# Raw weight loads, the residual load and unit spacing moved; the norm root of the next block multiplied in by GpSimd

## The chip, the cores and the metric

The kernel runs on one core of a Trainium2 chip. The metric is the device time of one execution in microseconds (us). The core has five engines that take their instructions in order, each from its own queue, and meet only through semaphores: TensorE (PE: matmuls, with a separate weight load, PEld), VectorE (DVE), ScalarE (ACT), GpSimd (POOL) and SyncE (SP). SP issues nearly all DMA transfers here; POOL issues some.

## The reference

One layer over 2048 tokens of width 1024, all in float32. A first RMS norm feeds one projection. Part of its columns goes through a diagonal state-space layer (S5), part through attention over 64-frame chunks; then come an output projection with residual, a second RMS norm with a SwiGLU block, a residual and a last norm.

```python
h = rmsnorm(x, norm_mix_g)                    # x * rsqrt(mean(x*x)) * g
proj = h @ w_in                               # u_ssm | q | k | v
y_ssm = s5_mixer(u_ssm, ...)                  # 32 groups, one 64-dim complex state each
y_att = chunked_attention(q, k, v, rel_bias)  # own chunk and 8 earlier ones, 8 heads
x = x + concatenate([rmsnorm(y_ssm), rmsnorm(y_att)]) @ w_out
h2 = rmsnorm(x, norm_ffn_g)
x = x + (silu(h2 @ w_gate) * (h2 @ w_up)) @ w_down
return rmsnorm(x, norm_final_g)
```

## The kernel before

Every float32 operand of a large product is split into a high and a low part (`split`, line 154: ACT copies the high part, DVE subtracts), and three matmuls make one product (`mm3`, line 148). So each operand that TensorE reads has passed ACT and DVE first. A tile framework allocates buffers by tag (a tag with `bufs=2` has two), sets all semaphores and orders each engine's queue: an instruction may go ahead of one that stands earlier in the program when it is ready and the earlier one is not, and program order decides between ready ones. TensorE's own order is pinned to program order (`Ordered`, line 72).

The stages, in order of time: the first projection and the S5 tables (`u_phase`); attention and the S5 scan together (`att_phase`); GLU and output projection (`mix_phase`); gate and up products (`gate_up_phase`, by a seven-product Strassen-like scheme); the down product (`down_phase`, the same scheme).

**The attention stage** runs over 128 steps `s`, 32 for each block of 512 tokens (`sb`). At each step TensorE gets the scores of one head's quarter of a block, the transposes of the step two earlier and, at the end of a head, its product with v (and a rescaling). Then every `Unit` in a list is advanced. A unit is a generator spread over steps `s0` to `s1`: it does its first part `pre` steps ahead of `s0` and the others evenly after that (`Unit.advance`, line 663). There are units for

- the next block's normed input (`hT_unit`, line 702): load the columns of x (`xt`, tag `xt` with 2 buffers of one tile, or tag `raw` with 2 buffers of two tiles), multiply by gain and norm root `rsn` (line 727, DVE), high part (728, ACT), low part (729, DVE). Tiles 0 to 2 have double buffers and come in a first unit (`HTA`), tiles 3 to 7 in a second one (`HTS`) when the previous block's last projection is through with them;
- the q/k and v projections (`qk_unit`, `v_unit`). Their weights come from `load_w` (line 684): in block 0 raw from the input, split, and the parts written out to `ws` (`keep_w`); in later blocks the parts are read back from `ws`;
- the S5 scan, eight units of 4 groups (`ssm_unit`, line 557), one after the other. Each has 42 parts: 18 loads by SP (U, Bst, Tm, Vm), idle parts, the input product (line 585; TensorE, into `pj`, from U and Bst; ACT copies it to X), the scan on POOL (lines 602 to 605 and 613, 614; one chain in which each instruction needs the one before), the DMA XG by POOL's queue (636), idle parts, and the output product (line 645), which reads XG and after which U's buffer is free for the next unit.

S5 unit b stood at steps 2 + 15b to 2 + 15(b + 1). `HTA` and `HTS` are counted from the block's first step, `HTP` is the `pre` of the second unit.

**The down stage** takes groups of 3 (or 2) row tiles. For each of the seven products of a group, `operand` (line 1487) loads h and w (768 KB each) by SP, splits them, and 36 matmuls run; then DVE adds four banks to the accumulator `acc` (line 1513), which starts as the residual, read from `x1` (`load_acc`, line 1515, 4 MB for a half of the tokens, right after the first product's operands).

Of the kernel before, what the change touches and what calls it, by code (L numbers as in the profile page):

```python
# [10 lines left out]
F32R = mybir.dt.float32r  # L11
I32 = mybir.dt.int32
AF = mybir.ActivationFunctionType
ALU = mybir.AluOpType
# [35 lines left out]
SW = 15  # L50
CUT = -8, -2, 2, 7, 13, 19, 24
CUTL = -8, -2, 2, 7, 13, 19, 23
ORDER = "sptf"
# [18 lines left out]
class Ordered:  # L72


    def __init__(self, tc):
        self.tc = tc
# [20 lines left out]
def f32(ap):  # L97
    return ap.bitcast(F32)
# [55 lines left out]
def split(k, hi, lo, raw):  # L154
    nc = k.nc
    return nc.scalar.copy(hi, raw), nc.vector.tensor_tensor(lo, raw, f32(hi), op=ALU.subtract)  # L156
# [499 lines left out]
class Unit:  # L656


    def __init__(self, gen, n, s0, s1, pre=0, done=0, light=1):
        self.gen, self.n, self.s0, self.s1, self.pre, self.done = gen, n, s0, s1, pre, done  # L660
        self.room = lambda a, b: sum(light if s % 4 == LPH else 1 for s in range(a, b))

    def advance(self, s):

        if s < self.s0 - self.pre:
            return
        want = 1
        if s >= self.s0:
            want += math.ceil((self.n - 1) * self.room(self.s0, s + 1) / self.room(self.s0, self.s1) - 1e-9)
        if s >= self.s1 - 1:  # L670
            want = self.n + 1
        while self.done < want:
            self.done += 1
            if next(self.gen, self) is self:
                self.done = 1 << 30


def att_phase(k, ident, S, aw, x0, roots):

    tc, nc, io, pfs = k.tc, k.nc, k.io, k.pfs  # L680
    with ExitStack() as cx:
        hT, vts, qk, keep = {0: tuple(zip(*x0))}, {}, {}, {}

        def load_w(sb, n):

            w = k.t(aw, "w", [P, 2, 1024], F32R, bufs=WB)
            if sb == 0:
                raw = k.t(aw, "raw", [P, 1024], bufs=2)
                nc.sync.dma_start(raw[:], io["w_qk"][n] if n < 8 else io["w_v"][n - 8])
                for ins in split(k, w[:, 0], w[:, 1], raw[:]):  # L690
                    if n in (0, 4):
                        k.tc.keep_in_program_order(ins)
                keep[n] = w
            else:
                nc.sync.dma_start(f32(w[:]), S["ws"][n])
            return w[:, 0], w[:, 1]

        def keep_w(n):
            if n in keep:
# [2 lines left out]
        def hT_unit(sb, q0=0, q1=KT):  # L702
            hi, lo = hT.setdefault(sb, ([], []))
            ts = slice(sb * SB, (sb + 1) * SB)
            xts = {}

            def load(q, n=1):
                t = k.t(aw, "raw", [P, 1024], bufs=2) if n > 1 else k.t(aw, "xt", [P, SB], bufs=XB)
                nc.sync.dma_start(t[:].rearrange("p (q t) -> p q t", q=n), io["xt"][q * P : (q + n) * P, ts].rearrange("(q p) t -> p q t", p=P))
                for m in range(n):  # L710
                    xts[q + m] = t[:, m * SB : (m + 1) * SB]

            if q0 == 0:
                load(0)
                load(1)
            else:
                load(q0)
                for q in range(q0 + 1, q1, 2):
                    load(q, 2)
            for q in range(q0, q1):  # L720
                yield
                if q0 == 0 and q + 2 < q1:
                    load(q + 2)
# [3 lines left out]
                nc.vector.scalar_tensor_tensor(xt, xt, k.gm[:, q : q + 1], S["rsn"][:, ts], op0=ALU.mult, op1=ALU.mult)  # L727
                nc.scalar.copy(hi[q], xt)
                nc.vector.tensor_tensor(lo[q], xt, f32(hi[q]), op=ALU.subtract)
            yield  # L730

        def qk_unit(sb, pr):
            ws = [load_w(sb, n) for n in (pr, 4 + pr)]
            yield
            hi, lo = hT[sb]
            if (sb, pr) == (0, 0):
# [43 lines left out]
        QK_N = 1 + 2 * KT  # L780

        def v_unit(sb, fh):
            ws = [load_w(sb, 8 + 2 * r + fh) for r in range(2)]
# [143 lines left out]
        for sb in range(NSB):  # L927
            g0 = sb * 32
            C = CUT if sb < NSB - 1 else CUTL
            if sb > 0:  # L930
                if DB:
                    units.append(Unit(hT_unit(sb, 0, DB), 2 + DB, g0 + HTA[0], g0 + HTA[1], 2))
                units += [Unit(hT_unit(sb, DB), 2 + KT - DB, g0 + HTS[0], g0 + HTS[1], HTP), Unit(qk_unit(sb, 0), QK_N, g0 + C[0], g0 + C[1], 3, light=LIGHT)]
            units.append(Unit(v_unit(sb, 0), V_N, g0 + C[1], g0 + C[2], 2, light=LIGHT) if sb else Unit(v0, V_N, *V0, done=1))
            units += [ Unit(qk_unit(sb, 1), QK_N, g0 + C[2], g0 + C[3], 2, light=LIGHT),
                      Unit(qk_unit(sb, 2), QK_N, g0 + C[3], g0 + C[4], 2, light=LIGHT), Unit(v_unit(sb, 1), V_N, g0 + C[4], g0 + C[5], 2, light=LIGHT),
                      Unit(qk_unit(sb, 3), QK_N, g0 + C[5], g0 + C[6], 2, light=LIGHT)]
        for b in range(NG // GB):
            units.append(Unit(ssm_unit(k, sp, psum, S, b, k.ssm_eng), SSM_N, 2 + int(SW * b), 2 + int(SW * (b + 1)), light=SL))
        N = len(steps)  # L940
        for s in range(N + LAG + 2):
            if s == OPEN:
# [532 lines left out]
def down_phase(k, S):  # L1475
    tc, nc, io = k.tc, k.nc, k.io
    V, te = nc.vector, k.te
    with ExitStack() as cx:
# [5 lines left out]
        def bank(pool):  # L1484
            return k.t(pool, "ps", [P, 512])

        def operand(src, early=False):

            g, n = src.shape[0], src.shape[2]
            t = k.t(next(ring), "hd", [P, 2 * DG * 512], F32R)  # L1490
            hi, lo = (t[:, m * g * n : (m + 1) * g * n].rearrange("p (g c) -> p g c", g=g) for m in range(2))
            with tc.high_priority() if early else ExitStack():
                nc.sync.dma_start(f32(lo), src.rearrange("g p c -> p g c"))
            split(k, hi, lo, f32(lo))
            return hi, lo

        def group(hf, f0, g, acc, early):

            fs = slice(f0, f0 + g)
            x, y = [bank(dx) for _ in range(4)], None  # L1500
            for n, on_x, first, r, c in ((B11, 1, 1, 0, 0), (T1, 0, 1, 1, 1), (T2, 1, 0, 0, 1), (B22, 0, 0, 0, 1), (T3, 1, 0, 1, 1), (B21, 0, 1, 0, 0), (T4, 1, 0, 1, 0)):
                h = operand(S["hq"][hf, fs, n], early and n in (B11, T1))
                w = operand(S["wc"][fs, n], early and n in (B11, T1))
                if n == B11 and f0 == 0:
                    load_acc(hf, acc)
# [9 lines left out]
        def load_acc(hf, acc):  # L1515
            for i in range(KT):
                a = k.t((a0, a1)[hf], f"acc{i}", [P, HALF])
                nc.sync.dma_start(a[:], S["x1"][i * P : (i + 1) * P, hf * HALF : (hf + 1) * HALF])
                acc.append(a)

        def down(hs, ds, tiles, acc, t0, tn, end):

# [174 lines left out]
```

## Time and profile before

| | |
|---|---|
| time, median of 3 runs | 2295.97 us (2287.0 to 2296.15) |
| the profiled execution's own time | 2289.1 us |
| its span in the profile | 2287.1 us |
| mean granted TensorE clock | 0.978 |
| attention stage | about 130 to 690 us of the span |
| output projection, gate and up | to about 1831 us |
| down stage | 1831 us to the end |

In the profile, an engine's busy time leaves out what its queue does while it waits. "Idle before" an instruction is the time its engine had nothing to run, and the name behind the arrow is what ended it. "x8" is the number of instructions in the row. A name such as `pj<-XG,Vm` is output and inputs by the program's names. Rows of the table by stretches give each engine's busy time, the granted TensorE clock (1.00 is full), the busy share of the 16 DMA engines and GB/s. In the chain of waits each row has its start, its length, and what the chain ran through.

### The profile page before, as it was taken

The page shows a single profiled execution, that of the slowest core. Times are in us where ns is not written, and L with a number is a line of the kernel's source. Part 1 is how long each engine was busy: PE and PEld are TensorE (multiplying, and loading weights), DVE is VectorE, ACT ScalarE, POOL GpSimd, SP SyncE. Part 2 cuts the span into 40 slices and gives each one's busy share as a digit, 9 for nine tenths or more (in the row PEclk, how much of TensorE's full clock was granted, in tenths as well). Part 3 has the DMA queues.
Part 4 walks back from the last instruction along what each step waited for, and adds up shares of the span by engine and source line. Part 5 has one row for each costly group of instructions (what it writes and reads, how often), then busy time and mean ns, then how long its engine had stood idle before and what let it go on. Part 6 is the DMA issues. An engine that isn't in the chain of part 4 may idle for free.

```text
span 2287.1 us, 30278 instructions
## 1 busy us (share of the span) xinstructions
PE 2171.6 (95%) x10632; PEld 1830.1 (80%) x10632; DVE 1544.7 (68%) x2695; ACT 1000.6 (44%) x1654; POOL 348.7 (15%) x813
## 2 busy tenths in 40 slices
PE   8988899999996899999999999999999989999997
PEld 6777688898985788878888887888888778888886
DVE  7755565555556766876776678666666477789776
ACT  6444555455557652343333335333333343344322
POOL 2245765455660000000000000000000000000000
PEclk9998999999998999999999999999999999999999
DMA  8767886666644534854465567555423297465552
GB/s 299 236 221 220 257 223 201 187 188 179 188 132 124 171 121 147 267 189 151 160 200 178 167 211 258 203 169 188 139 96 110 78 341 252 166 212 193 206 189 74
DMA packets 215256, 428.33 MB, mean 187 GB/s; under 512 B 38592, under 2 KB 61168, under 8 KB 208000
## 3 DMA queue, kind: packets, MB, share of 16 engines
q1 hardware_dynamic: 210368, 412.50, 55.3%
q0 software_dynamic: 4736, 13.91, 2.0%
q8 instruction: 83, 1.36, 0.2%
q14 instruction: 69, 0.57, 0.1%
HBM read 286.86 MB, written 129.00 MB: 182 GB/s over the span
## 4 chain that ended last, share of the span: by engine, by line
PE 80%; DVE 6%; DMA 4%; POOL 4%; issue 3%; ACT 1%; SPq 1%; DVEq 0%; POOLq 0%; ACTq 0%
PE X L79 20%; PE ps L79 19%; PE Y L79 10%; PE pf L79 9%; PE big L79 9%; PE W L79 5%; PE pj L79 4%; PE sc L79 2%; PE pt L82 2%; DMA xt<-in_xp 1%; DMA hd<-wc 1%; POOL X L605 1%; DVE lo L156 1%; POOL X L604 1%; POOL st L602 1%
## 5 line engine op out<-in xcount | busy, mean ns | idle before, releaser
L79 PE MATMUL X<-hi,c 128*128 128x512 f32 x1408 | 451.0, 391 | 6.9 <-DVE c L156 5.4
L79 PE MATMUL ps<-hd,hd 128*128 128x512 f32 (+1 forms) x1968 | 430.8, 381 | 6.1 <-ACT hd L156 4.5
L79 PEld LDWEIGHTS ps<-hd,hd 128*128 128x128 f32 x1968 | 358.0, 189 | 77.7 <-ACT hd L156 5.3
L79 PEld LDWEIGHTS X<-hi,c 128*128 128x128 f32 x1408 | 265.3, 189 | 63.4 <-DVE c L156 6.3
L79 PE MATMUL X<-lo,c 128*128 128x512 f32 x704 | 274.9, 391 | 0.0
L156 ACT CAST hd<-hd 128x1536 fp32r<-128x1536 f32 (+1 forms) x106 | 147.7, 1393 | 236.3 <-DMA hd<-hq 178.7
L79 PE MATMUL Y<-hi,c 128*128 128x512 f32 x704 | 224.7, 390 | 1.5 <-DVE u L1389 1.5
L156 DVE TENSOR_TENSOR hd<-hd 128x1536 fp32r<-128x1536 f32 (+1 forms) x106 | 174.4, 1646 | 29.1 <-ACT hd L156 28.4
L156 DVE TENSOR_TENSOR c<-S,c 128x512 fp32r<-128x512 f32 x176 | 121.0, 689 | 98.3 <-ACT c L156 98.0
L1385 ACT COPY u<-X 128x512 f32<-128x512 f32 x132 | 77.4, 587 | 200.7 <-PE X L79 200.7
L1513 DVE TENSOR_TENSOR acc<-acc,ps 128x512 f32<-128x512 f32 x196 | 130.9, 684 | 50.3 <-PE ps L79 47.8
L156 ACT CAST c<-S 128x512 fp32r<-128x512 f32 x176 | 109.4, 622 | 120.1 <-PE Y L79 61.6
L79 PE MATMUL pf<-hi,w 128*128 128x512 f32 x416 | 153.9, 422 | 8.4 <-ACT w L156 4.7
L79 PE MATMUL big<-m,woh 128*128 128x512 f32 x512 | 161.2, 396 | 0.0
L79 PEld LDWEIGHTS Y<-hi,c 128*128 128x128 f32 x704 | 132.5, 188 | 29.9 <-DVE u L1389 2.2
L79 PEld LDWEIGHTS X<-lo,c 128*128 128x128 f32 x704 | 132.8, 189 | 27.5
L156 ACT CAST c<-raw 128x512 fp32r<-128x512 f32 x132 | 82.3, 623 | 150.5 <-PE Y L79 68.5
L79 PE MATMUL Y<-lo,c 128*128 128x512 f32 x352 | 137.2, 390 | 0.0
L868 DVE TENSOR_TENSOR ptl<-pt,pth 128x640 fp32r<-128x640 f32 (+3 forms) x152 | 98.3, 647 | 47.5 <-ACT pth L867 45.9
L852 ACT ACTIVATE s<-s,mn 128x640 f32<-128x640 f32 (+4 forms) x128 | 98.0, 765 | 65.6 <-DVE mn L849 61.1
L867 ACT CAST pth<-pt 128x640 fp32r<-128x640 f32 (+3 forms) x152 | 83.8, 551 | 95.6 <-PE pt L82 91.5
L79 PE MATMUL W<-hi,c 128*128 128x512 f32 x352 | 115.5, 389 | 0.0
(441 smaller groups left out, 4169.9 us busy)
## 6 DMA issues: line engine op xcount, KB each, us to landing
w<-wss SPq DMA_DIRECT2D x36, 1024.0 KB, 6.0
hq<-g SPq DMA_DIRECT2D x140, 256.0 KB, 2.1
hd<-hq SPq DMA_DIRECT2D x42, 768.0 KB, 4.5
hd<-wc SPq DMA_DIRECT2D x42, 768.0 KB, 6.0
raw<-in_w_gate SPq DMA_DIRECT2D x44, 512.0 KB, 3.8
raw<-in_w_up SPq DMA_DIRECT2D x44, 512.0 KB, 4.3
wc<-px SPq DMA_DIRECT2D x66, 256.0 KB, 3.2
wss<-w SPq DMA_DIRECT2D x12, 1024.0 KB, 5.7
```

Source lines behind the costliest of these rows:

```text
L79: return self.tc.keep_in_program_order(self.tc.nc.tensor.matmul(*a, **b))
L82: return self.tc.keep_in_program_order(self.tc.nc.tensor.transpose(*a, **b))
L156: return nc.scalar.copy(hi, raw), nc.vector.tensor_tensor(lo, raw, f32(hi), op=ALU.subtract)
L602: eng.tensor_tensor(t[:, :, :, :n], src, ar, op=ALU.mult)
L604: eng.tensor_tensor(dst, dst, t[:, :, :, :n], op=ALU.add)
L605: eng.tensor_tensor(dst, dst, t2[:, :, :, :n], op=ALU.add)
L852: nc.scalar.activation(s[:, :nk], s[:, :nk], AF.Exp, bias=mn[:], scale=-1.0, accum_out=sums[sb, pr][:, hh, qp : qp + 1])
L867: nc.scalar.copy(pth[:, a:b, qp, :], pt[:, a:b, :])
L868: nc.vector.tensor_tensor(ptl[:, a:b, qp, :], pt[:, a:b, :], f32(pth[:, a:b, qp, :]), op=ALU.subtract)
L1385: nc.scalar.copy(u[:], ps[:])
L1513: V.tensor_tensor(a, a, ps[:], op=ALU.add)
```

## The change

Five things change together.

1. Block 0's q/k and v weights: the raw loads move to a part of their own, 4 steps ahead of the unit in place of 2; the split stays 2 steps ahead (`mid=2`).
2. The S5 units' spacing: `SU` in place of 15 steps each.
3. The next block's input: POOL multiplies by `rsn` (a part of its own for tiles 3 to 7, 2 steps ahead); ACT makes the high part with the gain as its scale; DVE makes the low part as (x times gain) minus high. DVE's first multiplication goes.
4. The loads for it: the first unit starts 3 steps earlier, the second unit's loads stand 5 steps ahead in place of 2.
5. The down stage: in the first group of each half, a product's operands are loaded one product ahead, and `acc` is loaded in four quarters, each ahead of the product that first adds to it. In the very first group the operands are issued by POOL's queue (`aside`).

```diff
-HTA = -12, -9
+HTA = -15, -12
-HTP = 2
+HTP = 5
-SW = 15
+SU = 2, 19, 35, 49, 64, 78, 93, 107, 122
 class Unit:
-        want = 1
+        want = 1 if self.mid is None or s < self.s0 - self.mid else 2
         if s >= self.s0:
-            want += math.ceil((self.n - 1) * self.room(...) / ...)
+            want += math.ceil((self.n - want) * self.room(...) / ...)
+        def load_ws(sb, ns):
+            raws = [load_raw(n) for n in ns] if sb == 0 else []
+            if raws and ns not in ((0, 4), (8, 10)):
+                yield
...
 def hT_unit
+            def norm(q):
+                nc.gpsimd.tensor_tensor(xts[q], xts[q], S["rsn"][:, ts], op=ALU.mult)
...
+                yield
+                for q in range(q0, q1):
+                    norm(q)
...
-                nc.vector.scalar_tensor_tensor(xt, xt, k.gm[:, q : q + 1], S["rsn"][:, ts], op0=ALU.mult, op1=ALU.mult)
-                nc.scalar.copy(hi[q], xt)
-                nc.vector.tensor_tensor(lo[q], xt, f32(hi[q]), op=ALU.subtract)
+                nc.scalar.activation(hi[q], xt, AF.Copy, scale=k.gm[:, q : q + 1])
+                nc.vector.scalar_tensor_tensor(lo[q], xt, k.gm[:, q : q + 1], f32(hi[q]), op0=ALU.mult, op1=ALU.subtract)
...
-            units.append(Unit(ssm_unit(...), SSM_N, 2 + int(SW * b), 2 + int(SW * (b + 1)), light=SL))
+            units.append(Unit(ssm_unit(...), SSM_N, SU[b], SU[b + 1], light=SL))
...
 def operand
-                nc.sync.dma_start(f32(lo), src.rearrange("g p c -> p g c"))
+                (nc.gpsimd if aside else nc.sync).dma_start(f32(lo), src.rearrange("g p c -> p g c"))
 def group
+            if f0 == 0:
+                acc += [k.t((a0, a1)[hf], f"acc{i}", [P, HALF]) for i in range(KT)]
+                load(0)
+            for m, (n, on_x, first, r, c) in enumerate(order):
+                load(m + 1 if f0 == 0 else m)
+                if f0 == 0 and (r, c) not in seen:
+                    seen.add((r, c))
+                    load_acc(hf, acc, r, c)
...
-                nc.sync.dma_start(a[:], S["x1"][i * P : (i + 1) * P, hf * HALF : (hf + 1) * HALF])
+                nc.sync.dma_start(acc[i][:, c * 512 : (c + 1) * 512], S["x1"][i * P : (i + 1) * P, cs])
```

More of the change, by code (lines that the diff above doesn't have):

```diff
@@ L656, with __init__ @@
 class Unit:
-    def __init__(self, gen, n, s0, s1, pre=0, done=0, light=1):
-        self.gen, self.n, self.s0, self.s1, self.pre, self.done = gen, n, s0, s1, pre, done
+    def __init__(self, gen, n, s0, s1, pre=0, done=0, light=1, mid=None):
+        self.gen, self.n, self.s0, self.s1, self.pre, self.done, self.mid = gen, n, s0, s1, pre, done, mid
         self.room = lambda a, b: sum(light if s % 4 == LPH else 1 for s in range(a, b))
@@ L682, in att_phase, with load_raw @@
         hT, vts, qk, keep = {0: tuple(zip(*x0))}, {}, {}, {}
[L684 to L696, printed above, removed]
+        def load_raw(n):
+            raw = k.t(aw, "raw", [P, 1024], bufs=2)
+            nc.sync.dma_start(raw[:], io["w_qk"][n] if n < 8 else io["w_v"][n - 8])
+            return raw
+        def load_ws(sb, ns):
+            raws = [load_raw(n) for n in ns] if sb == 0 else []
+            if raws and ns not in ((0, 4), (8, 10)):
+                yield
+            ws = []
+            for i, n in enumerate(ns):
+                w = k.t(aw, "w", [P, 2, 1024], F32R, bufs=WB)
+                if raws:
+                    for ins in split(k, w[:, 0], w[:, 1], raws[i][:]):
+                        if n in (0, 4):
+                            k.tc.keep_in_program_order(ins)
+                    keep[n] = w
+                else:
+                    nc.sync.dma_start(f32(w[:]), S["ws"][n])
+                ws.append((w[:, 0], w[:, 1]))
+            return ws
         def keep_w(n):
@@ L719, in hT_unit @@
                     load(q, 2)
+                yield
+                for q in range(q0, q1):
+                    norm(q)
             for q in range(q0, q1):
                 yield
-                if q0 == 0 and q + 2 < q1:
-                    load(q + 2)
+                if q0 == 0:
+                    if q + 2 < q1:
+                        load(q + 2)
+                    norm(q)
                 xt = xts[q]
@@ L726, in hT_unit @@
                     v.append(k.t(aw, f"{n}{q}x" if q < DB and sb % 2 else f"{n}{q}", [P, SB], F32R)[:])
-                nc.vector.scalar_tensor_tensor(xt, xt, k.gm[:, q : q + 1], S["rsn"][:, ts], op0=ALU.mult, op1=ALU.mult)
-                nc.scalar.copy(hi[q], xt)
-                nc.vector.tensor_tensor(lo[q], xt, f32(hi[q]), op=ALU.subtract)
+                nc.scalar.activation(hi[q], xt, AF.Copy, scale=k.gm[:, q : q + 1])
+                nc.vector.scalar_tensor_tensor(lo[q], xt, k.gm[:, q : q + 1], f32(hi[q]), op0=ALU.mult, op1=ALU.subtract)
             yield
         def qk_unit(sb, pr):
-            ws = [load_w(sb, n) for n in (pr, 4 + pr)]
+            ws = yield from load_ws(sb, (pr, 4 + pr))
             yield
@@ L782, in v_unit @@
         def v_unit(sb, fh):
-            ws = [load_w(sb, 8 + 2 * r + fh) for r in range(2)]
+            ws = yield from load_ws(sb, (8 + fh, 10 + fh))
             yield
@@ L1485, in bank, with operand @@
             return k.t(pool, "ps", [P, 512])
-        def operand(src, early=False):
+        def operand(src, early=False, aside=False):
             g, n = src.shape[0], src.shape[2]
@@ L1499, in group, with load @@
             fs = slice(f0, f0 + g)
+            order = (B11, 1, 1, 0, 0), (T1, 0, 1, 1, 1), (T2, 1, 0, 0, 1), (B22, 0, 0, 0, 1), (T3, 1, 0, 1, 1), (B21, 0, 1, 0, 0), (T4, 1, 0, 1, 0)
             x, y = [bank(dx) for _ in range(4)], None
[L1501 to L1505, printed above, removed]
+            ops = {}
+            def load(m):
+                if m < len(order):
+                    n = order[m][0]
+                    soon = early and n in (B11, T1)
+                    ops[n] = operand(S["hq"][hf, fs, n], soon, early), operand(S["wc"][fs, n], soon, early)
+            if f0 == 0:
+                acc += [k.t((a0, a1)[hf], f"acc{i}", [P, HALF]) for i in range(KT)]
+                load(0)
+            seen = set()
+            for m, (n, on_x, first, r, c) in enumerate(order):
[3 more added lines that the diff above has]
+                    load_acc(hf, acc, r, c)
+                h, w = ops.pop(n)
                 if not on_x and first:
@@ L1513, in group, with load_acc @@
                     V.tensor_tensor(a, a, ps[:], op=ALU.add)
[L1515 to L1519, printed above, removed]
+        def load_acc(hf, acc, r, c):
+            for i in range(4 * r, 4 * r + 4):
+                cs = slice(hf * HALF + c * 512, hf * HALF + (c + 1) * 512)
+                nc.sync.dma_start(acc[i][:, c * 512 : (c + 1) * 512], S["x1"][i * P : (i + 1) * P, cs])
         def down(hs, ds, tiles, acc, t0, tn, end):
```

11 lines of the change are left out of this document (5 added, 6 removed).

## The prediction

> **What bounds the kernel now.** I read the page first, then the chain of waits through the attention stage, the busy time by stretches, and the timelines at TensorE's idle times.
>
> ```profile
> span 2287.1 us, 30278 instructions
> PE 80%; DVE 6%; DMA 4%; POOL 4%; issue 3%; ACT 1%; SPq 1%; DVEq 0%; POOLq 0%; ACTq 0%
> ```
>
> TensorE carries the chain for 80% of the span; what an edit here can win lies in the other fifth. GpSimd is in it, though the kernel as a whole hardly uses it. The chain says where; its rows are start, length, what:
>
> ```profile
> 158.78 1.73 PE pj L79 x8
> 162.85 0.51 POOL st L602
> 205.53 1.21 POOL XG L636 x2
> 206.74 24.57 issue
> 274.60 6.93 DMA XG<-X
> 292.56 5.74 DMA U<-u
> 300.04 1.13 PE pj L79 x4
> 348.86 3.47 PE pj L79 x16
> 423.22 3.45 PE pj L79 x16
> ```
>
> From 162.85 to 274.60 the chain doesn't run through TensorE. It runs through POOL's scan of S5 unit 0, then that of unit 1, then XG's transfer; then it waits for unit 2's load of U, which can't start before unit 1's output product has freed the buffer. The 24.57 us called "issue" are POOL with nothing to do until unit 1's input product. So the first three units form a loop of their own: input product (X), scan, XG, output product (Y), loads, X. TensorE's order is pinned, so it waits where it comes to Y or X too early:
>
> ```profile
> 173.01 0.79 PE L79 MATMUL pf<-hi,w 128*128 128x512 f32 x1 [4.67 <-ACT w L156]
> 193.50 0.87 PE L82 MATMUL pt<-ident,s 128*128 128x128 f32 x3 [3.36 <-DVE ptl L868]
> 212.53 0.67 PE L79 MATMUL pj<-XG,Vm 128*128 128x256 f32 x2 [1.68 <-DMA XG<-X]
> 252.30 0.50 PE L79 MATMUL pf<-hi,w 128*128 128x512 f32 x1 [3.15 <-ACT hi L728]
> 364.46 0.89 PE L79 MATMUL pj<-U,Bst 128*128 128x256 f32 x3 [3.00 <-DMA Tm<-kts]
> 411.87 0.69 PE L82 MATMUL pt<-ident,s 128*128 128x128 f32 x2 [3.80 <-DVE ptl L868]
> ```
>
> The bracket is TensorE's idle time and what ended it. The idle times at 173, 193, 252 and 411 are those that the change goes for: block 0's split weights, and the next block's input. But after those at 173 and 193 TensorE still came 1.68 us too early for XG at 212.53: what they cost was time it would have waited anyway. Only from X3 (364.46) on does TensorE set the pace.
>
> **The change, part by part.** The sum is made against the profiled execution's own 2289.1 us (span 2287.1); the median of the three runs, 2295.97, is 6.9 above it, and the result is given against that median.
>
> *Spacing.* A unit's 42 parts are dealt out by `Unit.advance`: X are parts 9 and 10, Y 41 and 42. By its formula X stood in steps 4, 19, 34, 49, 64... (both parts) and Y in 16, 31, 46, 61, 76...; now X is in 4 and 5, 21 and 22, 37, 51, 66, 80, 95, 109 and Y in 18, 34, 48, 63, 77, 92, 106, 121. While the loop sets the time, that moves work of TensorE into its waits: X3 comes two steps later in the work. A step costs (348.86 - 300.04) / 12 = 4.07 us, from unit 2, in which TensorE had no idle time: -8.1. Against it, scans 0 and 1 start a step later, as their second part does. A step of block 0 is (212.53 - 158.78 - 4.67 - 3.36 - 1.68 - 6.9) / 12 = 3.1 us, where 6.9 is lost to the half clock after the first two idle times (8 us at a mean of 0.57 each):
>
> ```profile
> 172.00:180.00 8.00, 6.95 (x20) 5.28 (x21) 3.60 (x6) 2.91 (x7) 7.53 (x13) 0.57 0.71 255
> ```
>
> The row is one stretch: its length, the busy time of PE, PEld, DVE, ACT and POOL with their instructions, the granted clock, the share of the DMA engines and GB/s. So +6.2, and together -1.9.
>
> *Raw weights* (173, 193) and the idle time at 252 gone: 4.67 + 3.36 + 6.9 and some 7 us with the clock. All of it lies before Y0 or Y1, which the scans hold: TensorE would reach step 18 near 202, and XG can't be there before 216 (the old 158.78 to 213, a step later). I take 0. What is late next is XG. The eight or so loads of weights that move ahead on SP (0.44 us each by the median of line 709's raw loads, below) pass stores that nobody near waits for; the wait at Y0 hides them too, and without it they would cost 2 to 4 us.
>
> *Unit 4 and 6* have 11 steps from X to Y in place of 12.
>
> ```profile
> 482.64 1.21 POOL L636 DMA_DIRECT2D XG<-X  x2 [0.30 <-POOL X L614]
> 490.26 0.59 PE L79 MATMUL pj<-XG,Vm 128*128 128x256 f32 x2
> DMA to landing us min/median/max: 2.4/4.6/7.9
> ```
>
> The last row is that of all XG transfers. With its median, unit 4's XG was there 490.26 - 482.64 - 1.21 - 4.6 = 1.8 us ahead; 4.07 us less leaves a wait of 2.3. Unit 6 I put between this and unit 3 (6.5 ahead, below), at 0.5: +2.8.
>
> *The norm root on POOL*: 24 instructions of 128x512 that the trace doesn't have.
>
> ```profile
> L614 POOL TENSOR_TENSOR X<-X,fx 128x434 f32<-128x434 f32 x32 | 35.3, 1104 | 2.1
> L727 DVE SCALAR_TENSOR_TENSOR raw<-raw,g_mix,rsn 128x512 f32<-128x512 f32 x12 | 12.0, 1027 | 0.5 <-DMA raw<-in_xt 0.5
> L727 DVE SCALAR_TENSOR_TENSOR xt<-xt,g_mix,rsn 128x512 f32<-128x512 f32 x12 | 9.0, 764 | 8.8 <-DMA xt<-in_xt 8.8
> L709 SPq DMA_DIRECT2D xt<-in_xt x12: 332/426/1372, 207.4 to 398.2; - x12
> L709 SPq DMA_DIRECT2D raw<-in_xt x6: 426/440/1423, 242.6 to 398.6; - x6
> ```
>
> By size, 1104 x 512 / 434 gives 1.30 us each, 31 us on POOL for 21 us off DVE. The Trainium skill, GPSIMD Engine Reference, section 3.1, puts a two-input instruction at about 2.6 cycles an element at 1.2 GHz; an estimate from it is 1.1 us for 512, with which the sum would be 2 us lower.
>
> Where they run matters more. The loads show it: block 3's last ones went out at 398.6, though their place in the program is step 86; between step 49 (X3, 364.46) and step 61 (Y3, 423.22) that time is step 56. So they go out when a buffer comes free, not at their step, and moving them three or more steps ahead moves only block 1's, which wait for the raw buffers of block 0. The norms will follow them as DVE's did (214.6 to 408.5 for line 727). POOL's scan is one chain, and a ready instruction of lower rank can slip in between its links. Block 1's eight fall between scans 0 and 1: 0 lost, and DVE's nine multiplications no longer run beside scan 1, which was slow:
>
> ```profile
> 227.00:283.00 56.00, 44.95 (x230) 36.93 (x231) 31.88 (x75) 28.63 (x74) 40.74 (x88) 0.94 0.80 246
> 300.00:349.00 49.00, 48.84 (x297) 43.91 (x298) 32.93 (x57) 29.46 (x58) 37.82 (x88) 1.00 0.80 246
> 364.00:424.00 60.00, 53.47 (x285) 47.01 (x286) 41.23 (x65) 32.26 (x64) 40.17 (x88) 0.91 0.69 211
> 642.00:691.00 49.00, 46.51 (x296) 42.53 (x297) 26.08 (x49) 26.95 (x56) 34.98 (x88) 0.97 0.47 131
> ```
>
> Column six is POOL's busy time for the same 88 instructions: 40.74 in unit 1, 34.98 in unit 7. Between 0 and -5.8 I take -3. Block 2's: three in the pause, five inside scan 2 (+6.5; -1 for less disturbance): +5.5, all paid, as the loop holds there. Block 3's: seven inside scan 3 (9.1, less 2.6 of the 5.2 that 40.17 lies over 34.98): 6.5.
>
> *The idle time at 411* was DVE's, whose line 727 held up line 868; gone, it frees 3.80 and about 3.4 of half clock, 7.2. In unit 3 XG's last issue started at 411.43; landed by the median that is 416.7, 6.5 ahead of Y3 at 423.22. The norms use these 6.5 up, and TensorE then waits for XG the 7.2 that it gained: 0.
>
> ```profile
> 411.43 0.63 POOL L636 DMA_DIRECT2D XG<-X  x1 [0.30 <-POOL X L614]
> L728 ACT CAST hi<-raw 128x512 fp32r<-128x512 f32 x12 | 7.2, 616 | 3.6 <-DVE raw L727 3.4
> L446 ACT ACTIVATE hi<-xt,g_mix 128x512 fp32r<-128x512 f32 x16 | 11.0, 716 | 7.9 <-DMA xt<-in_xp 7.9
> ```
>
> *Loads and splits.* Block 1's three transfers now stand ahead of unit 1's 18 loads in SP's queue, on the loop: between 3 x 0.43 and 3 x 1.4 us, I take +2. ACT's scaled form costs 0.10 us more a tile (716 against 616), five tiles at each of three handovers: +1.5. Nothing waits behind the new norms on POOL but the scan and XG.
>
> *The down stage.*
>
> ```profile
> 1831.56 5.88 SPq L1518 DMA_DIRECT2D acc<-x  x8
> 1837.58 0.44 SPq L1493 DMA_DIRECT2D hd<-hq  x1
> 1852.12 1.22 PE L79 MATMUL ps<-hd,hd 128*128 128x512 f32 x2 [2.70 <-ACT hd L156]
> 1853.91 1.65 PE L79 MATMUL ps<-hd,hd 128*128 128x512 f32 x3 [0.57 <-DVE hd L156]
> 1831.00:1850.00 19.00, 16.90 (x72) 13.36 (x72) 10.68 (x12) 4.66 (x4) 0.00 (x0) 1.00 1.03 393
> 1850.00:1859.00 9.00, 6.31 (x15) 4.53 (x16) 7.11 (x6) 6.75 (x6) 0.00 (x0) 0.62 1.05 408
> ```
>
> The third product's operands queue behind 4 MB of residual, with all DMA engines busy (1.03). Loading a quarter (1 MB) first and the operands one product ahead takes out 2.70 + 0.57 and the half clock (9 us at 0.62: 3.4), -6.7. POOL's queue may bring the first operands later or not at all later; I take +1: -5.7. The Trainium skill, Trainium Kernel Development and Optimization, section Key Constraints, says that queues share the same 16 DMA engines and a second queue saves issue time alone; by it the gain is the order of the bytes, which the share of 1.03 agrees with, and POOL's queue adds 0.
>
> Sum: -1.9 + 0 + 2.8 - 3 + 5.5 + 0 + 2 + 1.5 - 5.7 = +1.2 us: 2290.3 for the profiled execution, 2297 against the median.
>
> **Rivals.**
>
> *The pauses take the norms* (faster). A pause of POOL like that of 24.57 us holds 8 x 1.30 us. If all norms fall there and the scans calm down to unit 7's: -1.9 + 2.8 - 5.8 - 2.8 (37.82 to 34.98) - 7.2 (scan 3 is then 5.2 shorter, so Y3 doesn't wait) + 0 + 1.5 - 6.7 = -20: 2276. Against it: the loads go out during scans 2 and 3.
>
> *The scan pays* (slower). A norm stands in POOL's queue ahead of the scan's next link and waits for its transfer, as DVE did (8.8 us in three waits, line 727's row). With half of that in each of scans 2 and 3 and no calming: -1.9 + 2.8 + 0 + (6.5 + 4.4) + (9.1 + 4.4 - 6.5 = 7.0, and 3.4 of half clock) + 4.2 + 1.5 - 5.7 = +22: 2318. It decides from where scans 2 and 3 grow by some 10 us more than the 12 above. For it: these loads are the ones that landed late. The Trainium skill's GPSIMD Engine Reference, section 4.1, tells to keep elementwise work on VectorE, which points the same way.
>
> *The plain reading*: every idle time named is won, 14.9 + 7 + 7.2 + 6.7 = 36: 2260. The chain speaks against it.
>
> **How the numbers follow.** Forecast 0.43, pauses 0.21, scan pays 0.31, plain reading 0.05. 0.5% (11.5 us) is about what a measurement of this kernel can tell from no change. The forecast's own spread is 2286 to 2308; it gives 0.37 within, 0.03 on each side. The pauses give 0.19 faster, 0.02 within; the scan 0.29 slower, 0.02 within; the plain reading 0.05 faster. So 0.27, 0.41, 0.32. The range 2275 to 2319 takes in both rivals' values and leaves out the plain reading and what lies beyond them, under 0.2.
>
> **What would show it.** Right: idle times at 173, 193, 252 and 411 gone or small, and in their place waits of `pj<-XG,Vm` for XG at Y0 (over 8 us), Y1 and Y2; norms between lines 602 and 614 in scans 2 and 3; no idle time over 1 us between the down stage's second and third product. Wrong: Y0 to Y2 without waits (then the loop was shorter than I think, and the plain reading gains), scans of about 35 us throughout, or an idle time of POOL inside a scan that a transfer of x ends.

## The result and the profile after

| | kernel before | changed kernel |
|---|---|---|
| median, run beside each other | 2296.15 us (2282.42 to 2302.85, 7 runs) | 2307.29 us (2300.44 to 2311.63, 7 runs) |
| ratio, with its 95% interval | | 1.0056 (1.0036 to 1.0076) |
| ratio, measured a second time, with other runs of both | | 1.0066 (1.0044 to 1.0087) |

The change costs 11 to 15 us. The forecast was +1; 2307 lies in the range of 2275 to 2319, but on the slow side of the 0.5% that the prediction called no change.

The profiled executions differ by more, 2309.9 against 2289.1 us. They were granted different clocks, 0.974 and 0.978. A second profile of the changed kernel was granted 0.978, took 2299.2 us, and so compares better. By stage, from the first rows of `sc<-hi2x,hi0x`, `pf<-gh,wgh` and `ps<-hd,hd` and the span (the attention stage runs here up to the first GLU product, some 25 us further than in the table of the kernel before):

| us | before (0.978) | changed (0.974) | changed, second profile (0.978) |
|---|---|---|---|
| attention stage | 132.40 to 714.56: 582.2 | 134.20 to 736.58: 602.4 | 131.46 to 731.16: 599.7 |
| from there to the down product | 1116.9 | 1119.1 | 1114.3 |
| down stage to the end | 455.6 | 452.4 | 451.9 |

The loss is in the attention stage, 17 to 20 us; the down stage gains 3 to 4. Single traces scatter by some us: the stages between these two, which the change leaves as they were, took 1114.3 to 1120.9 us in the fourteen traces of this document, and two kernels with the same attention stage took 582.2 and 578.3 us for it. The page of the changed kernel, its span and its chain by engine:

```profile
span 2308.1 us, 30358 instructions
PE 72%; POOL 7%; DVE 6%; issue 5%; DMA 4%; ACT 1%; SPq 1%; DVEq 0%; POOLq 0%; ACTq 0%
```

TensorE carries 72% of the chain in place of 80%, GpSimd 7% in place of 4%. The chain through the attention stage (start, length, what) says where:

```profile
212.53 1.29 POOL xt L722
246.09 3.36 issue
354.02 20.82 issue
415.86 1.29 POOL xt L722
417.93 5.86 DVE lo1x L744
428.79 41.76 issue
508.17 6.74 DMA XG<-X
```

The two long rows called issue (354.02 and 428.79) are POOL with nothing to do until the next unit's input product. The new norm (line 722) is in the chain itself, and around 416 us the chain goes from the norm into `lo1x` on DVE. `lo1x` is the low part of tile 1 of block 3, which TensorE doesn't read before step 88 of the 128. TensorE was at step 59 then. TensorE's idle times in the changed kernel:

```profile
171.62 0.44 PE L82 MATMUL pt<-ident,s 128*128 128x128 f32 x2 [3.20 <-DVE ptl L883]
215.27 0.67 PE L79 MATMUL pj<-XG,Vm 128*128 128x256 f32 x2 [3.75 <-POOL xt L722]
235.25 2.04 PE L79 MATMUL pj<-U,Bst 128*128 128x256 f32 x4 [5.51 <-DMA Tm<-kts]
426.06 1.33 PE L82 MATMUL pt<-ident,s 128*128 128x128 f32 x5 [22.74 <-DVE ptl L883]
515.04 1.19 PE L79 MATMUL pj<-XG,Vm 128*128 128x256 f32 x2 [5.26 <-DMA XG<-X]
```

At 173, 193 and 252 us the old idle times are gone or smaller, and waits for XG and for unit 1's tables stand in their place, as forecast. (The bracket at 215.27 names the norm that POOL ran just then; by the trace the third of XG's four transfers landed at 215.03.) What was not forecast is one idle time of 22.74 us where 3.80 had been (the old one at 411). Up to step 58 the changed kernel is 4.7 us ahead; at step 60 it is 14.2 us behind. The three other engines over that stretch (start, length, engine, line, instruction; in brackets the idle time before it and what ended it), POOL first:

```profile
413.30 1.04 POOL L614 TENSOR_TENSOR X<-X,fx 128x434 f32<-128x434 f32 x1
414.63 1.21 POOL L636 DMA_DIRECT2D XG<-X  x2 [0.30 <-POOL X L614]
415.86 2.50 POOL L722 TENSOR_TENSOR xt<-xt,rsn 128x512 f32<-128x512 f32 x2
418.30 4.92 POOL L722 TENSOR_TENSOR raw<-raw,rsn 128x512 f32<-128x512 f32 x4
417.17 0.72 ACT L743 ACTIVATE hi1x<-xt,g_mix 128x512 fp32r<-128x512 f32 x1 [20.45 <-POOL xt L722]
417.80 0.81 ACT L867 ACTIVATE s<-s,mn 128x640 f32<-128x640 f32 x1
417.93 5.85 DVE L744 SCALAR_TENSOR_TENSOR lo1x<-xt,g_mix,hi1x 128x512 fp32r<-128x512 f32 x1 [19.22 <-ACT hi1x L743]
423.70 0.74 DVE L744 SCALAR_TENSOR_TENSOR lo2x<-xt,g_mix,hi2x 128x512 fp32r<-128x512 f32 x1
425.18 0.82 DVE L883 TENSOR_TENSOR ptl<-pt,pth 128x640 fp32r<-128x640 f32 x1
```

Read it from the top. POOL is in scan 3 until XG's last issue at 414.63, and the next instruction in its queue is block 3's norm. ACT's queue had reached `hi1x`, which needs that norm, and stood there for 20.45 us. Behind it in the same queue were the exponential of the scores (line 867) and the high part of the transposes (line 882), which were needed at once. DVE stood 19.22 us at `lo1x`, with `ptl` (line 883) three places behind it. TensorE waited for `ptl`. When the norm came, `lo1x` took 5.85 us for what takes 0.74 us one row below, while POOL's four norms of `raw` ran beside it. The price by stretches (length; busy time of PE, PEld, DVE, ACT, POOL; granted clock; DMA share; GB/s):

```profile
402.00:426.00 24.00, 1.33 (x10) 1.03 (x8) 8.01 (x5) 3.91 (x7) 20.00 (x26) 0.61 0.14 29
426.00:432.00 6.00, 5.93 (x21) 5.06 (x21) 3.48 (x8) 2.10 (x4) 1.29 (x1) 0.55 1.02 301
515.00:522.00 7.00, 6.96 (x23) 5.84 (x24) 0.56 (x1) 1.17 (x2) 0.00 (x0) 0.63 0.05 11
```

In the first 24 us POOL works almost alone. The 6 us after it run at a clock of 0.55, which costs 2.7 us more. The third row is the half clock after the wait at unit 4's output product (515.04), 2.6 us of 7.

The order of the queues shows that this is not chance. The order is written when the kernel is built: behind scan 0's last XG issue stand 8 norms, behind scan 1's 8, behind scan 2's 1, behind scan 3's 7. Not one of the 24 stands inside a scan. So the scans were not disturbed by them; they became shorter. Scans 1 to 3, before and then changed, 88 instructions each:

```profile
231.20:275.60 44.40, 35.39 (x176) 28.59 (x175) 29.48 (x66) 23.15 (x60) 40.54 (x88) 0.92 0.79 251
304.20:345.60 41.40, 41.40 (x247) 37.02 (x247) 29.60 (x51) 24.86 (x48) 37.58 (x88) 1.00 0.85 263
368.70:412.40 43.70, 37.81 (x217) 33.55 (x216) 34.11 (x52) 23.71 (x45) 39.92 (x88) 0.95 0.75 238
```

```profile
244.80:285.20 40.40, 36.44 (x228) 32.73 (x226) 22.79 (x58) 21.98 (x59) 36.54 (x88) 0.96 0.84 257
313.90:352.50 38.60, 38.00 (x250) 34.78 (x249) 24.29 (x44) 23.42 (x46) 34.74 (x88) 1.00 0.78 239
374.80:415.85 41.05, 26.19 (x150) 22.63 (x148) 18.62 (x30) 16.43 (x30) 37.26 (x88) 0.90 0.64 194
```

POOL's busy time fell from 40.54, 37.58 and 39.92 us to 36.54, 34.74 and 37.26. DVE's first multiplication, which is gone, explains a part of it. With the norm back on DVE and the new spacing kept (the first experiment) scans 1 and 3 take 39.15 and 39.77 us, so its share there is 2.6 and 2.5; scan 2 takes 34.77, as without it (34.74). With the spacing alone scan 2 takes 35.11: it is the spacing that made this one shorter.

In the down stage, the idle time of 2.70 us ahead of the third product and the half clock after it are gone. The timeline has two idle times left there, both inside the first product; the stretches over the first three products follow, at a clock of 1.00 in place of 0.62:

```profile
1856.31 0.50 PE L79 MATMUL ps<-hd,hd 128*128 128x512 f32 x1 [0.23 <-DVE hd L156]
1858.58 7.76 PE L79 MATMUL ps<-hd,hd 128*128 128x512 f32 x33 [1.77 <-DVE hd L156]
```

```profile
1855.00:1874.00 19.00, 17.00 (x74) 13.55 (x73) 16.71 (x16) 5.93 (x4) 6.08 (x8) 1.00 1.04 411
1874.00:1883.00 9.00, 9.00 (x42) 7.44 (x41) 7.56 (x7) 4.45 (x3) 1.52 (x2) 1.00 1.04 416
```

### The profile page after: what moved, and what is told of

Same layout as the page of the kernel before. It is cut to its first block, busy times and chain, and to the rows that moved or that the text cites. A ratio compares the mean times of both kernels' runs of the same rounds, so it can differ in the third digit from the quotient of the medians.

```text
span 2308.1 us, 30358 instructions
## 1 busy us (share of the span) xinstructions
PE 2172.7 (94%) x10632; PEld 1830.1 (79%) x10632; DVE 1530.8 (66%) x2671; ACT 1002.5 (43%) x1654; POOL 383.6 (17%) x851
## 4 chain that ended last, share of the span: by engine, by line
PE 72%; POOL 7%; DVE 6%; issue 5%; DMA 4%; ACT 1%; SPq 1%; DVEq 0%; POOLq 0%; ACTq 0%
PE X L79 19%; PE ps L79 17%; PE Y L79 10%; PE big L79 8%; PE pf L79 7%; PE W L79 5%; PE pj L79 3%; PE sc L79 1%; POOL X L605 1%; PE pt L82 1%; POOL X L604 1%; POOL X L614 1%; POOL st L602 1%; POOL st L603 1%; DMA hd<-wc 1%
## 5 line engine op out<-in xcount | busy, mean ns | idle before, releaser
L1507 POOL DMA_DIRECT2D hd<-hq x7 | 5.3, 764 | 1136.8 <-PE X L79 1123.1
```

## The experiments

Three theories. **A**: ACT and DVE stand at the high and low parts of a later block, because these wait for norms that POOL takes up only after its scan. **B**: the spacing costs, by unit 4's 11 steps. **C**: the norms' own time on POOL lengthens the scans. Ratios are to the kernel before, run on the same chip, with 95% intervals.

| kernel | ratio | interval |
|---|---|---|
| parts 1, 2, 5: norm on DVE as before | 1.0015 | 0.9999 to 1.0031 |
| parts 3, 4 alone: norm on POOL | 1.0191 | 1.0166 to 1.0216 |
| changed, block 3 on DVE | 0.9986 | 0.9971 to 1.0001 |
| part 5 alone: down stage | 0.9968 | 0.9953 to 0.9984 |
| changed, ACT's order of block 3 pinned | 1.0082 | 1.0068 to 1.0097 |
| changed, 12 steps for units 4 and 6 | 1.0055 | 1.0042 to 1.0067 |
| part 1 alone: raw weights | 1.0020 | 1.0006 to 1.0033 |
| part 2 alone: spacing | 1.0025 | 1.0009 to 1.0041 |
| changed, again | 1.0066 | 1.0044 to 1.0087 |
| changed, block 3 on DVE, 12 steps | 0.9971 | 0.9956 to 0.9985 |
| the same with the raw weights as before | 0.9988 | 0.9973 to 1.0002 |
| parts 2 and 5 with 12 steps | 0.9977 | 0.9961 to 0.9993 |

**The norm back on DVE.** `hT_unit`, its loads and `HTA`, `HTP` as before; the rest changed.

```diff
-                nc.gpsimd.tensor_tensor(xts[q], xts[q], S["rsn"][:, ts], op=ALU.mult)
...
-                nc.scalar.activation(hi[q], xt, AF.Copy, scale=k.gm[:, q : q + 1])
...
+                nc.vector.scalar_tensor_tensor(xt, xt, k.gm[:, q : q + 1], S["rsn"][:, ts], op0=ALU.mult, op1=ALU.mult)
+                nc.scalar.copy(hi[q], xt)
...
```

> The changed kernel with parts 3 and 4 undone: the next block's input is multiplied by DVE in one instruction with the gain, and its loads stand where they stood before. Raw weights, spacing and down stage stay changed. Theory A (ACT and DVE stand behind POOL): the changed kernel's one idle time of 22.74 us of TensorE at 426 is gone and some 2.7 us of half clock after it, an idle time of about 4 us by DVE's multiplication comes back: 2307 - 22.7 - 2.7 + 4 = about 2286, that is 10 below the kernel before. Theory B (the spacing costs: unit 4's 11 steps): the wait for XG of 5.26 us at unit 4's output product and its half clock stay, and the norm was worth little: 2303 to 2307. Theory C (norms lengthen the scans and XG): not more than 5 us gained, and scans 2 and 3 shorter than the 35.6 and 37.9 us of busy time with the norm on POOL.

Measured 2292.52 us, ratio 1.0015: 0.4% below the changed kernel. The 22.74 us are gone; an idle time of 2.48 us stands at 407.69. That is less of a gain than theory A's 10 us below the kernel before: the wait for XG at unit 4 (4.54 us at 499.05) stayed, as theory B says, and unit 0's output product waited 9.07 us. Theory C falls: with the norm back on DVE, scans 1 and 3 are longer, not shorter, and scan 2 is the same. Scans 1 to 3:

```profile
240.80:283.80 43.00, 33.96 (x184) 28.83 (x183) 27.26 (x63) 21.90 (x57) 39.15 (x88) 0.88 0.77 254
313.80:352.40 38.60, 36.29 (x234) 32.80 (x233) 24.10 (x41) 21.64 (x42) 34.77 (x88) 1.00 0.74 229
376.70:420.30 43.60, 37.52 (x203) 31.94 (x202) 34.66 (x54) 25.48 (x49) 39.77 (x88) 0.96 0.76 232
```

**The norm alone on POOL.** The opposite edit, made in the kernel before.

```diff
...
+                nc.gpsimd.tensor_tensor(xts[q], xts[q], S["rsn"][:, ts], op=ALU.mult)
...
```

> The kernel before with parts 3 and 4 alone: norm on POOL, loads three steps further ahead. Theory A: an idle time of TensorE of about 20 us near 410 to 430 us, with ACT's queue standing at the high part of block 3's second tile: 2296 + 20 + 2 less the 3.80 us at 411 and its half clock = about 2311. Theory B: no loss, 2293 to 2297, as the units keep their 12 steps. Theory C: scans 1 to 3 longer by 5 us and more, 2300 to 2306, and no single idle time over 8 us in the attention stage.

Measured 2334.6 us, ratio 1.0191: 44 us, three times theory A's number. Theory A had counted one stall. With the old spacing there are three, one for each block. TensorE's rows, then ACT's at the second and third:

```profile
260.00 0.44 PE L79 MATMUL sc<-k,q2h 128*128 128x128 f32 x1 [17.38 <-issue]
358.42 1.33 PE L82 MATMUL pt<-ident,s 128*128 128x128 f32 x5 [22.23 <-DVE ptl L875]
451.00 1.33 PE L82 MATMUL pt<-ident,s 128*128 128x128 f32 x5 [13.44 <-DVE ptl L875]
356.21 0.72 ACT L735 ACTIVATE hi<-xt,g_mix 128x512 fp32r<-128x512 f32 x1 [23.21 <-POOL xt L714]
448.65 0.72 ACT L735 ACTIVATE hi1x<-xt,g_mix 128x512 fp32r<-128x512 f32 x1 [15.85 <-POOL xt L714]
```

Block 2's norms now stood behind scan 2, not behind scan 1, and ACT waited 23.21 us for the first of them. Block 1's last five had been put inside scan 1; at the first stall ACT waited 6.27, 4.38 and 2.55 us for norms of that block, with `k`, which TensorE missed, behind them in its queue. So the other parts of the changed kernel hide two of three such stalls: there the norms of blocks 1 and 2 stand directly behind scans 0 and 1. That it is the spacing that does this, by units 1 and 2 being later, fits the order but was not tested by itself.

**Block 3 on DVE.** POOL still does blocks 1 and 2.

```diff
+                if sb == NSB - 1:
+                    nc.vector.scalar_tensor_tensor(xt, xt, k.gm[:, q : q + 1], S["rsn"][:, ts], op0=ALU.mult, op1=ALU.mult)
+                    nc.scalar.copy(hi[q], xt)
+                    nc.vector.tensor_tensor(lo[q], xt, f32(hi[q]), op=ALU.subtract)
+                    continue
```

> The changed kernel, but the last block's input (eight tiles, needed some 140 us after the stall) is multiplied by DVE as before; POOL still does blocks 1 and 2. Theory A: the stall at 426 goes with these eight tiles alone, for it was their high parts that stood at the head of ACT's queue: about 2284 to 2288. If instead block 2's tiles, normed by POOL after scan 1, are what TensorE misses there: about 2307, as the changed kernel. Theory B: 2303 to 2307.

Measured 2288.56 us, ratio 0.9986, in the range that theory A gave. Eight of 24 tiles account for the whole loss, 0.7%, about 16 us. Where 22.74 us had been, and at ACT's same instruction:

```profile
406.94 0.77 PE L82 MATMUL pt<-ident,s 128*128 128x128 f32 x5 [2.48 <-DVE ptl L889]
400.76 0.60 ACT L746 CAST hi1x<-xt 128x512 fp32r<-128x512 f32 x1
```

ACT makes `hi1x` at 400.76 with no idle time before it.

**The down stage alone.**

```diff
...
+            load(m + 1 if f0 == 0 else m)
...
+                    load_acc(hf, acc, r, c)
...
```

> The kernel before with part 5 alone (the down stage's loads). The trace of the changed kernel shows 7 us less of lost time between 1815 and 1860 us: by that 2296 - 7 = 2289. Rival: the order of loads only moves the wait to a later product or to the end of the stage: 2294 to 2297.

Measured 2282.84 us, ratio 0.9968, that is -7.3 us (-10.8 to -3.7); the two medians differ by 5.5. The stage from its first product to the end took 451.8 us against 455.6. In the nine other traces with the edit it took 451.5 to 452.4, in three more without it 456.1 to 457.0. So the stage itself shows 3 to 6 us. In this pair of traces another 3.9 us lie in the attention stage, which the edit doesn't touch; the gain is shown, its size only to within the interval.

**ACT's order pinned.** All norms stay on POOL; ACT takes block 3's high parts at their own place in the program.

```diff
-                nc.scalar.activation(hi[q], xt, AF.Copy, scale=k.gm[:, q : q + 1])
+                ins = nc.scalar.activation(hi[q], xt, AF.Copy, scale=k.gm[:, q : q + 1])
+                if sb == NSB - 1:
+                    k.tc.keep_in_program_order(ins)
```

> The changed kernel with one thing more: ACT takes the eight high parts of the last block at their own place in the program and not earlier. POOL still makes all 24 norms, at the same places of its queue as far as scan 3 goes. Theory A (what costs is that ACT's queue, and DVE's behind it, stands at block 3's high parts while POOL scans): the idle time of 22.74 us at 426 goes, though the norms run where they ran: 0.4% to 0.8% under the changed kernel's 1.0056, so a ratio to the kernel before of 0.996 to 1.001. Rival (the norms' own time on POOL, or their running beside DVE): the ratio stays at 1.004 to 1.007.

Measured 2308.66 us, ratio 1.0082. By the number, theory A missed. The trace says why: the stall at 426 did go (TensorE's idle times over 1.2 us leap from 390 to 441), but another of 20.73 us came two scans later. The edit did more than it was meant to: two norms had moved with their high parts, from behind scan 3 to between the last links of scan 5 in POOL's queue. ACT stood at the high part that needs the first of them:

```profile
540.12 1.26 POOL L722 TENSOR_TENSOR xt<-xt,rsn 128x512 f32<-128x512 f32 x1
541.41 0.72 ACT L743 ACTIVATE hi2x<-xt,g_mix 128x512 fp32r<-128x512 f32 x1 [22.45 <-POOL xt L722]
542.17 0.75 DVE L746 SCALAR_TENSOR_TENSOR lo2x<-xt,g_mix,hi2x 128x512 fp32r<-128x512 f32 x1 [20.95 <-ACT hi2x L743]
544.43 1.33 PE L82 MATMUL pt<-ident,s 128*128 128x128 f32 x5 [20.73 <-DVE ptl L885]
```

The same chain at another time: POOL's norm at the end of a scan, ACT 22.45, DVE 20.95, TensorE 20.73. A single tile is enough. Here `lo2x` took 0.75 us, as no norm stood directly behind the first one, so the wait for the scan is the main part of a stall and the slow `lo1x` the smaller one. The four norms of `raw` stayed directly behind scan 3 and stopped nobody there.

**Twelve steps for unit 4.**

```diff
-SU = 2, 19, 35, 49, 64, 78, 93, 107, 122
+SU = 2, 19, 35, 49, 64, 79, 94, 108, 122
```

> The changed kernel with units 5, 6 and 7 one step later, so that units 4 and 6 have 12 steps from input to output product as before. Theories A and B together (both costs are there, and they add): the wait for XG of 5.26 us at unit 4's output product and the half clock behind it (about 3 us) go, the stall of 22 us at 426 stays: 8 us under the changed kernel, ratio 1.001 to 1.004. If B alone were the cause, 0.993 to 0.997; if spacing is worth nothing, 1.004 to 1.007.

Measured 2300.91 us, ratio 1.0055, outside what A with B expected. In its trace unit 4's output product does not wait, and the stall is still there (21.04 us at 423.05); its attention stage took 595.6 us, 4.1 less than the changed kernel's second profile and 6.8 less than its first, which is little more than the 3.9 by which equal stages differ. A new wait takes a part back: unit 5's input product stands 2.13 us for U, and 2.21 to 2.47 in the three later kernels with 12 steps. The time of the runs doesn't show the gain. The same step was taken twice more, below: from 0.9986 to 0.9971 with block 3 on DVE, and from the 0.9993 that parts 2 and 5 alone would make together to 0.9977. Three differences of 0 to -0.16%, each smaller than its intervals: unit 4's short stretch costs between nothing and some 4 us, and the size is not settled.

**Raw weights alone, spacing alone.**

```diff
...
-            ws = [load_w(sb, n) for n in (pr, 4 + pr)]
+            ws = yield from load_ws(sb, (pr, 4 + pr))
...
```

> The kernel before with part 1 alone (raw weights two steps earlier). By the loop of the first units the idle times at 173 and 193 go and TensorE waits as much longer for XG at unit 0's output product: within 3 us of the kernel before, ratio 0.999 to 1.001. Rival (the idle times were a true cost): 10 to 15 us gained, ratio 0.993 to 0.996.

Measured 2293.62 us, ratio 1.0020: neither a gain of 10 us nor quite zero. The mechanism is the one that was forecast: the idle time at 173 fell from 4.67 to 2.81, the one at 193 from 3.36 to 1.54, and unit 0's output product waited for XG 6.53 us in place of 1.68. The attention stage took 581.9 us, against 582.2. Scan 0 had 41.91 us of busy time against 39.93: the splits now run beside it. In this pair of traces the whole difference lies outside the attention stage, where the edit changes nothing, so the 0.2% has no cause that these traces show.

```diff
-            units.append(Unit(ssm_unit(...), SSM_N, 2 + int(SW * b), 2 + int(SW * (b + 1)), light=SL))
+            units.append(Unit(ssm_unit(...), SSM_N, SU[b], SU[b + 1], light=SL))
```

> The kernel before with part 2 alone (the units' spacing). Theory B: unit 4's 11 steps cost 8 us with the half clock, and the later unit 3 gives back at most 2: ratio 1.002 to 1.004, with a wait for XG of 4 to 6 us at unit 4's output product. By the prediction's terms (-1.9 + 2.8): 1.0004, so 0.999 to 1.002.

Measured 2294.01 us, ratio 1.0025, with a wait for XG of 4.57 us at unit 4's output product: theory B's numbers, and above the 0.999 to 1.002 by the prediction's terms. It is a small loss by itself, 6 us (2 to 9).

**Both mends, and what each part is worth in them.** The changed kernel once more, the changed kernel with block 3 on DVE and 12 steps, the same with the old raw weights, and the kernel before with parts 2 and 5 and 12 steps, side by side.

> The changed kernel as it is, beside the other three on one chip, as the measure for them: ratio to the kernel before 1.004 to 1.007, with the idle time of 20 to 23 us of TensorE near 426.

Measured 2306.29 us, ratio 1.0066, with the idle time of 22.64 us at 423.50.

> The changed kernel with both mends: the last block's input multiplied by DVE, and units 5 to 7 one step later (12 steps for unit 4). Theory A with B: both losses go, 1.0056 - 0.0070 - 0.0030 = 0.9956 (0.993 to 0.997), below the down stage's change alone (0.9968) or equal to it. If the 12 steps are worth nothing, as the ratio of the run with them alone says against its trace: 0.998 to 1.000.

Measured 2283.81 us, ratio 0.9971: faster than both kernels, 22 us below the changed one on the same chip. It lies between the two expectations: just short of the smallest gain that theory A with B allowed (0.997), and below the 0.998 to 1.000 of 12 steps that are worth nothing. It is level with the down stage's edit alone (0.9968), so the other four parts, mended, are worth nothing that these runs can tell.

```diff
...
-            ws = yield from load_ws(sb, (pr, 4 + pr))
+            ws = [load_w(sb, n) for n in (pr, 4 + pr)]
...
```

> The run above with block 0's raw weights loaded and split as before. By the prediction's step (what is gained at 173 and 193 us is waited for XG) it equals the run above within 0.15%. Rival (the earlier splits cost something of their own, as the ratio of 1.002 of that part alone says): 0.1% to 0.3% below it.

Measured 2286.85 us, ratio 0.9988. The rival is out: the old weights are not faster but 0.17% slower, just beyond the 0.15% of the step. The two intervals overlap (0.9956 to 0.9985 and 0.9973 to 1.0002), so the raw loads are worth zero to a few us here.

```diff
-SW = 15
+SU = 2, 19, 35, 49, 64, 79, 94, 108, 122
...
+            load(m + 1 if f0 == 0 else m)
...
```

> The kernel before with the down stage's change and the spacing with 12 steps for units 4 and 6; weights and norm as before. If the spacing without unit 4's short stretch is worth nothing, 0.996 to 0.998, as the down stage alone. The run above differs from it only by POOL's norms of blocks 1 and 2: theory A allows these to be a gain where they fall into POOL's pauses (DVE then leaves scan 1 alone), some 0.3% below this run; if every norm on POOL costs, this run is the faster.

Measured 2285.41 us, ratio 0.9977. The run above, which adds POOL's norms of blocks 1 and 2 (and part 4's earlier loads), is not below it but level (0.9988). So these norms in POOL's pauses cost nothing and bring nothing that shows; the 0.3% between the first and the third kernel of the table did not repeat.

## Why the prediction was right in its range and wrong in its reason

*The step that failed* is the norm on POOL, in four sentences of the prediction. "The norms will follow them as DVE's did", since "a ready instruction of lower rank can slip in between its links": the queue's order is written at build time, and in the changed kernel all norms were put behind the scans (in the kernel with the norm alone five stood inside scan 1, so that was not sure). The +5.5 for scan 2 was not paid. "TensorE then waits for XG the 7.2 that it gained: 0": scan 3 was shorter, and that wait did not come; but TensorE had just lost 19 us (4.7 ahead at step 58, 14.2 behind at step 60), so no run puts this step to the test. And "Nothing waits behind the new norms on POOL but the scan and XG" asked who waits behind the norm in POOL's queue, and not who waits for its result at the head of another engine's queue. There the price was: 22.74 + 2.7 of half clock, less 3.80 + 3.4 that the old idle time at 411 had cost, 18 us where the prediction had 0. Moving the eight tiles back to DVE gained 16.

*The rivals.* The likeliest case missed by 10 to 14 us. "The scan pays" had the sign, with 2318, and was wrong in its mechanism: scans 1 to 3 became shorter, and no idle time of POOL lies inside one. "The pauses take the norms" was right about where the norms run, and wrong about what that costs: a norm that keeps to a pause is late by up to a scan, and whoever was queued for it is late with it. The Trainium skill's rule against such work on GpSimd (GPSIMD Engine Reference, section 4.1) pointed the right way; the runs give it another reason than POOL's speed, since with the new spacing the norms of blocks 1 and 2 cost nothing that the runs can tell.

*The terms that held.* A norm took 1.28 us by the median of 12 (1.30 forecast from the scan's rows). The shorter scan 1 gave 40.54 - 36.54 = 4.0 us of busy time for 3, 2.6 of it by the norm. The idle times at 173, 193 and 252 were worth nothing that the runs can tell: TensorE met later waits at unit 0's output product (3.75 us) and unit 1's input product (5.51, for the table Tm; this is where the +2 for block 1's transfers ahead of unit 1's loads would show, and the old wait there was 1.45). The first was forecast at over 8; TensorE reached step 18 at 211.5 and not at 202, for transposes still waited 3.20 and 1.58 us and scores 1.15 us for DVE on the way. Of the two other waits for XG that were forecast, unit 1's output product waited 3.05 us and unit 2's not at all. The down stage was forecast at -5.7, the edit alone gave -7.3 (-10.8 to -3.7) by the runs, and a gain of 3 to 6 by the stage's own time.

*The term of the right kind and the wrong size* is unit 4: a wait of 2.3 us forecast, 5.26 measured, with 2.6 us of half clock behind it that the forecast had left out. XG's transfer, taken at its median of 4.6 us, took 6.7 there (508.17 in the chain). What that cost in the end is between nothing and 4 us, as said above. The +1.5 for ACT's scaled form could not be told apart in any run.

The sum missed by 10 to 14 us and not by 18, because 5.5 too much for scan 2 hid a part of what block 3 was short of. That the result lies in the range is luck: the range reaches up to 2319 for a rival whose mechanism did not come.

## What to carry to other kernels

When an operation moves to an engine that runs a long chain, ask two things: who is queued behind it there, and whose queue will stand at its first reader. Look where the reader stands in the compiled order of its engine: work for a far later block, put forward because its buffer is free, is harmless as long as its input comes from a prompt engine, and stops everything behind it when the input comes from a busy one. Here eight tiles, needed over 100 us later, cost 16 us; with them back on DVE the stall was gone.

## What the runs showed of the hardware

A DVE instruction with two inputs in SBUF took up to eight times its time while POOL ran large two-input instructions back to back. `lo1x` took 5.85 us beside four norms of `raw` (4.92 us in one row) and the end of the one before them, and 5.84 and 5.85 us at the same place in two other runs, where 0.74 us is its time with POOL quiet. Beside the short instructions of a scan the same form took 0.74 to 1.05 us in the changed kernel. The Trainium skill, SBUF — State Buffer, section Who interferes with whom, says that such an instruction contends with a GpSimd instruction that reads SBUF, because its second input comes through a read interface that the two engines share. The trace agrees for the norms, and here the wait went on over all four.
